# A transformer layer on one core: the first feed-forward input's last column groups in 512-column products, and the ada rows moved away from their end

## The chip, the cores and the metric

The kernel runs on one core of one Trainium2 chip. The core has a matrix engine (TensorE, PE in the profile, with its weight load shown as PEld), a vector engine (VectorE, DVE), a scalar engine (ScalarE, ACT), GpSimd (POOL) and the sync engine SyncE (SP), which here only issues DMAs. Each engine works through its own list of instructions in order and waits on semaphores of the others. The matrix engine writes only to PSUM, which this kernel uses as tiles of 128 x 512 fp32; everything else lies in SBUF.

The metric is the device time in microseconds of one execution. The profile is of one more execution; its times count from the first instruction.

## The reference

One layer, with 256 tokens of width 2048 and a feed-forward width of 5632:

```python
ada = (silu(c) @ w_ada + b_ada)
sh1, sc1, g1, sh2, sc2, g2, sh3, sc3, g3 = split(ada, 9)
h = swiglu(modulate(x, sh1, sc1), ffn1_w_in, ffn1_w_out)
x = layernorm(ALPHA * x + 0.5 * (1 + g1) * h, ln1_g, ln1_b)
h = token_mixer(modulate(x, sh2, sc2), ...)
x = layernorm(ALPHA * x + (1 + g2) * h, ln2_g, ln2_b)
h = swiglu(modulate(x, sh3, sc3), ffn2_w_in, ffn2_w_out)
x = layernorm(ALPHA * x + 0.5 * (1 + g3) * h, ln3_g, ln3_b)

def swiglu(h, w_in, w_out):
    gate, up = split(h @ w_in, 2)
    return (silu(gate) * up) @ w_out
```

Everything is fp32. The change is in the first `swiglu`, in its product with `ffn1_w_in` (2048 x 11264), and in when the pieces of `silu(c) @ w_ada` (2048 x 18432) are worked out.

## The kernel before

**Products in three parts.** Weights and activations are split into a high and a low part (`split`, L154 to L156: a cast on ACT gives the high part, a subtraction on DVE the low one), and a product is high x high + high x low + low x high. In `mm3` (L433) these are three matmuls into one PSUM range. With the weights as the stationary operand and 256 tokens as the moving one, each has 256 columns. In `mm2` (L439) the high weights meet the high and low activations, which lie side by side in one tile, in one matmul of 512 columns; its output fills a whole PSUM tile (high products left, low products right), and a second matmul of 256 columns adds low weights x high activations to the right half. Whoever empties such a tile must add the two halves.

**The first feed-forward's input.** `first_in` works out the first 12 of the 22 pairs of column groups in an order of its own. The other ten, of 256 gate and 256 up columns each, go through `ffn_in` (L458, called at L1075). Loop: group j from 12 to 21; in it gu = 0 (gate columns) and gu = 1 (up columns, called the value group here); `cols_form_a` (L444) then loads two pieces of 1024 x 256 weights (1 MB, `load_w`, one DMA on SP, raw buffer of three), splits each in two halves (six hi and six lo buffers), and issues the products, 8 k x 2 blocks for each piece. `outs[f].shape` decides between `mm2` and `mm3`. Without `values`, as at L1075, gate and up share two PSUM tiles of a group (256 columns each), and after both, silu on ACT (L474) and a multiplication on DVE (L475) empty them. With `values`, as in the second feed-forward (L1710), gate and up each take two whole tiles; a copy on ACT (L464) and an addition on DVE (L465) empty each, then follow silu (L488) for the gate and the multiplication (L485) for the up part. `values` is a pool with the place for the up part (tile u). `mm_tile` hands out five PSUM tiles in turn.

**The first feed-forward's output.** `out_proj` (L494) follows: columns 0 to 1023 in 22 units of two k, then twice 512 columns in 11 units of four k. The first pass needs four PSUM tiles. The last four units are loaded, but their products are held back for the boundary that follows (normalization, modulation, first products of the mixer).

**Ada rows.** `silu(c) @ w_ada` is worked out beside all this by `AdaQueue` (L219): a unit is 1024 columns in 16 rows; a row (`ada_rows`, L186) is a DMA of 128 x 1024 weights (0.5 MB, on SP's queue like the weights, two araw buffers) and one multiply-add on DVE (L170). After the sixteenth row comes a tail of five steps (splits, a sum over partitions on PE, L183, and the placing on DVE, L200 to L204 or L215). The next unit with the usual accumulator cannot begin while such a tail runs. The order is set by hand:

- `pump(n)`, called after a piece of weights, does one step of a tail and issues rows until what is owed is below one; n rows are added to what is owed.
- `half_step`, called by `load_w` between the two halves of a piece, issues half of the last pump's n ahead of time.
- `rest()` sets what is owed, and the rate, to zero.
- `need(n)` forces units until n are done.

The rates are R_F (first input, last quarter, nine pumps), R_IN (ffn_in), R_OUT (out_proj of the first feed-forward) and others (L814). Before the boundary after the first feed-forward `need(6)` (L1093) stands: gate 2 (two units) and shift and scale of the mixer (four). In the last value group the pumps are left out (`last`, L460) and made up for by two pumps behind the loop (L489); the rows of `half_step` still come in between. In the last four units of out_proj there are only steps of tails.

The tile framework orders the instructions of each engine by the program's order and its own estimates; `pinned()` keeps the ada rows behind certain instructions.

Of the kernel before, what the change touches and what calls it, by code (L numbers as in the profile page):

```python
# [9 lines left out]
AF = mybir.ActivationFunctionType  # L10
ALU = mybir.AluOpType
# [4 lines left out]
T = 256  # L16
# [16 lines left out]
def layer_kernel(  # L33
# [8 lines left out]
    V, S, G_, PE, SP = nc.vector, nc.scalar, nc.gpsimd, nc.tensor, nc.sync  # L42
# [23 lines left out]
    def fifth_tile(name):  # L66
        return pm.tile([P, 512], F32, tag="m5", name=name)

    def mm_tile(name, four=False):
        turn[0] = 0 if four else turn[0] % 5 + 1  # L70
        if turn[0] == 5:
            return fifth_tile(name)
        return pm.tile([P, 512], F32, tag="mm", bufs=4, name=name)
# [70 lines left out]
    pin = {}  # L144
# [74 lines left out]
    class AdaQueue:  # L219
# [55 lines left out]
        def pump(self, n):  # L275
            self.owed += n - self.given
            self.rate, self.given = n, 0
            self.end_step()
            self.owed_rows()
# [12 lines left out]
    ada = AdaQueue()  # L292
# [94 lines left out]
    def new_xT(tag):  # L387
        x = xp.tile([P, KD, 2, T], F32R, name=f"x_{tag}")
        return x[:, :, 0], x[:, :, 1], x


    def load_w(src, nk, w, name, by_parts=False, behind=None, into=None):
        raw = wp.tile([P, nk, w], F32, tag="raw", bufs=3, name=f"raw_{name}")
        src = src.rearrange("(k p) n -> p k n", p=P)
        if not by_parts:
            SP.dma_start(raw, src)
        h = nk // 2 if nk * w <= 2048 else nk // 4
        for q in range(nk // h):
            if by_parts:
                SP.dma_start(raw[:, q * h:(q + 1) * h], src[:, q * h:(q + 1) * h])  # L400
            if into:
                hi, los = into[q]
                S.copy(hi, raw[:, q * h:(q + 1) * h, :])
                n = h // len(los)
                for i, lo in enumerate(los):
                    pin["w"] = V.tensor_tensor(out=lo, in0=raw[:, q * h + i * n:q * h + (i + 1) * n, :],
                                               in1=hi[:, i * n:(i + 1) * n, :].bitcast(F32), op=ALU.subtract).ins
                for kk in range(h):
                    yield q * h + kk, hi[:, kk, :], los[kk // n][:, kk % n, :]
                continue  # L410
            if q:
                ada.half_step()
            hi = wp.tile([P, h, w], F32R, tag="hi", bufs=6, name=f"hi_{name}{q}")
            lo = wp.tile([P, h, w], F32R, tag="lo", bufs=6, name=f"lo_{name}{q}")
            with ExitStack() as s:
                if behind:
                    s.enter_context(tc.issue_after(behind))
                pin["w"] = split(raw[:, q * h:(q + 1) * h, :], hi, lo).ins
            for kk in range(h):
                yield q * h + kk, hi[:, kk, :], lo[:, kk, :]  # L420
# [6 lines left out]
    def unwoven(ps):  # L427
        return ps.rearrange("p (n a) -> p a n", a=2)

    def halves(v):  # L430
        return v.rearrange("p (a n) -> p a n", a=2)

    def mm3(o, ah, al, bh, bl, start, stop):  # L433
        bh, bl = woven(bh), woven(bl)
        PE.matmul(o, ah, bh, start=start, stop=False)  # L435
        PE.matmul(o, ah, bl, start=False, stop=False)  # L436
        PE.matmul(o, al, bh, start=False, stop=stop)  # L437

    def mm2(o, ah, al, x, start, stop):  # L439
        PE.matmul(o, ah, x.rearrange("p s (a n) -> p s n a", a=2), start=start, stop=False)  # L440
        PE.matmul(o[:, T:], al, woven(x[:, 0]), start=False, stop=stop)  # L441


    def cols_form_a(src, c0, outs, xT, name, npump, khs=(0, 1)):  # L444
        xhi, xlo, x = xT
        for kh in khs:
            for k8, hi, lo in load_w(src[kh * 1024:(kh + 1) * 1024, c0:c0 + 256], 8, 256, f"{name}_{kh}"):
                k = kh * 8 + k8
                for f in range(2):
                    fs = slice(f * P, (f + 1) * P)  # L450
                    start, stop = k == 8 * khs[0], k == 8 * khs[-1] + 7
                    if outs[f].shape[-1] == 2 * T:
                        mm2(outs[f], hi[:, fs], lo[:, fs], x[:, k], start, stop)
                    else:
                        mm3(outs[f], hi[:, fs], lo[:, fs], xhi[:, k, :], xlo[:, k, :], start, stop)
            npump()

    def ffn_in(w, xT, hT, j0, tag, npump, values=None):  # L458
        def one(j, gu, outs):
            last = gu and j == DFF // 256 - 1  # L460
            cols_form_a(w, gu * DFF + j * 256, outs, xT, f"{tag}i{j}_{gu}", (lambda: None) if last else npump)

        def both(dst, ps):
            S.copy(dst, unwoven(ps[:, :T]))  # L464
            V.tensor_tensor(out=dst, in0=dst, in1=unwoven(ps[:, T:]), op=ALU.add)  # L465

        for j in range(j0, DFF // 256):
            if values is None:
                ps = [mm_tile(f"gu_{tag}{j}_{f}") for f in range(2)]
                for gu in range(2):  # L470
                    one(j, gu, [p[:, gu * T:(gu + 1) * T] for p in ps])
                for f in range(2):
                    h = halves(hT[:, 2 * j + f, :])
                    S.activation(h, unwoven(ps[f][:, :T]), AF.Silu)  # L474
                    pin["h"] = V.tensor_tensor(out=h, in0=h, in1=unwoven(ps[f][:, T:]), op=ALU.mult).ins  # L475
                continue
            for gu in range(2):
                ps = [mm_tile(f"gu_{tag}{j}_{gu}{f}") for f in range(2)]
                one(j, gu, ps)
                for f in range(2):  # L480
                    h = halves(hT[:, 2 * j + f, :])
                    if gu:
                        u = halves(values.tile([P, T], F32, tag="u", bufs=2, name=f"u_{tag}{j}_{f}"))
                        both(u, ps[f])
                        pin["h"] = V.tensor_tensor(out=h, in0=h, in1=u, op=ALU.mult).ins  # L485
                    else:
                        both(h, ps[f])
                        S.activation(h, h, AF.Silu)  # L488
        for _ in range(2):  # L489
            npump()  # L490


# [312 lines left out]
    def entry_of(load, got, u0, u1):  # L805
        for u in range(u0, u1):
            got[u] = []
            for item in load(u):
                got[u].append(item)
                yield  # L810

    R_F, R_IN, R_OUT, R_MX, R_A, R_B = 1.25, 1.2, 1, 1.26, 1, .7  # L814
    NP = 2
    right = dict(side="right")
    def at(rate):
        return lambda: pump(rate)
# [18 lines left out]
    hT = Rows(hp, "hT1")  # L837
# [3 lines left out]
    xT = new_xT("f1")  # L841
    W1 = ffn1_w_in[0]
# [127 lines left out]
    NS = 12  # L970
# [99 lines left out]
    def first_hi_places(tag):  # L1070
        ent["hi0"] = tc.alloc_tile_pool(name=f"hi0{tag}", bufs=1)
        ent["hi"] = [ent["hi0"].tile([P, 2, T], F32R, name=f"hi{tag}_{k}") for k in range(0, 8, 2)]

    first_hi_places("1")
    ffn_in(W1, xT, hT, NS, "f1", at(R_IN))  # L1075
    xp.release()
    need(2)
    W = w_in[0]
# [58 lines left out]
    xT = new_xT("mx")  # L1137
    raws = [mo_raw(u) for u in range(3)]
    mow = {}
    fence, _, xs, ws = boundary(*ent["f"], ent["lgb"], 3, "1", xT, entry_of(mo_load, mow, 3, 6), KD, raws)  # L1140
# [14 lines left out]
    xhi, xlo, _ = xT  # L1155
# [83 lines left out]
    def form_a_four(c0, name, before_last=lambda: None):  # L1239
        ps = [mm_tile(f"pr_{name}{i}", True) for i in range(2)]  # L1240
        for u in range(4):
            if u == 3:
                before_last()
            for k4, hi, lo in load_w(W[u * 512:(u + 1) * 512, c0:c0 + 512], 4, 512, f"{name}{u}",
                                     behind=decays[0]):
                k = 4 * u + k4
                for f in range(4):
                    fs = slice(f * P, (f + 1) * P)
                    mm3(ps[f // 2][:, f % 2 * T:(f % 2 + 1) * T], hi[:, fs], lo[:, fs], xhi[:, k, :], xlo[:, k, :],
                        k + f % 2 == 0, k + f % 2 == KD)  # L1250
            decays[:] = decays[1], None
            step()
        return [ps[f // 2][:, f % 2 * T:(f % 2 + 1) * T] for f in range(4)]
# [279 lines left out]
    for i, c0 in enumerate((C_MQ, C_MK)):  # L1533
        ps = form_a_four(c0, f"m{i}")
# [82 lines left out]
    xT = new_xT("f2")  # L1617
# [13 lines left out]
    hT = Rows(hp, "hT2")  # L1631
# [46 lines left out]
    for us in (0, 1), (2,):  # L1678
        for q in QS:
            last = q == QS[-1]  # L1680
# [28 lines left out]
    vals = tc.alloc_tile_pool(name="vals2", bufs=1)  # L1709
# [45 lines left out]
```

## Time and profile before

| | us |
|---|---|
| median of three runs | 1869.42 |
| lowest and highest of them | 1862.72, 1870.07 |
| profiled execution | 1865.56 |
| its span, first to last instruction | 1863.9 |

The stages by the starts of their products in the trace: first input, first 12 groups, 34.6 to 306.4 us; its last ten groups (`ffn_in`, tiles gu_f, x_f, hi_f1i, lo_f1i) 306.4 to 523.5; the first output (tiles o_f, hi_f1o) 523.5 to 761; the mixer; the second input, of which `ffn_in` with `values` (hi_f2i) 1413.5 to 1624.9; the second output to the end.

How to read the rows: a group or timeline row names engine, line of kernel.py, operation, tiles as out<-in with buffer numbers left out, shape and count; in brackets or behind a bar stand the idle time of the engine just before and what ended it. A timeline row begins with its start and its length in us. A row by tile gives shortest, median and longest duration in ns, then the first and last start. The matmuls overlap, so a matmul's own duration is longer than the step from one to the next; the step is read from starts or from a stage's length.

### The profile page before, as it was taken

The numbers are of one execution on the slowest core, as the hardware profiler recorded it, in microseconds if no ns is written. First come the engines' busy times: TensorE is split into PE (matmuls) and PEld (weight loads), VectorE is DVE, ScalarE is ACT, GpSimd is POOL, SyncE is SP. The second block draws the span as 40 slices with busy tenths as digits, with TensorE's granted clock in tenths as the row PEclk, the third lists the DMA queues.
The fourth block names the chain that finished last, engine by engine and source line by source line (L and its number), as shares of the span: only waits on it lengthen the run. The fifth ranks groups of instructions, "written<-read, shape, count | busy, mean of one in ns | idle before, by whom it ended". The sixth has DMA issues, their size and how long they took to land.

```text
span 1863.9 us, 30963 instructions
## 1 busy us (share of the span) xinstructions
PE 1830.1 (98%) x12521; PEld 1694.2 (91%) x12521; DVE 1455.8 (78%) x1819; ACT 913.5 (49%) x1290; POOL 62.1 (3%) x92
## 2 busy tenths in 40 slices
PE   7999999999999999999999999999999999999997
PEld 5999999999988888689999887999999999988887
DVE  6889989778788787778889878777998776574655
ACT  3554454443454434655566645545454444554441
POOL 1211200000000000000000000000000000000000
PEclk9999999999999999999999999999999999999999
DMA  9989978999897889389978883998878876666663
GB/s 366 383 278 316 319 236 283 321 322 318 285 324 273 311 296 326 129 283 330 313 275 293 324 290 131 343 324 271 293 255 275 273 251 201 198 202 204 204 203 144
DMA packets 263431, 510.82 MB, mean 274 GB/s; under 512 B 10834, under 2 KB 93426, under 8 KB 262264
## 3 DMA queue, kind: packets, MB, share of 16 engines
q1 hardware_dynamic: 255176, 477.90, 74.9%
q0 software_dynamic: 8112, 30.95, 4.8%
q8 instruction: 98, 1.61, 0.4%
q14 instruction: 45, 0.37, 0.1%
HBM read 506.71 MB, written 2.10 MB: 273 GB/s over the span
## 4 chain that ended last, share of the span: by engine, by line
PE 56%; DVE 2%; DMA 1%; issue 1%; ACT 0%; POOL 0%; DVEq 0%; ACTq 0%; POOLq 0%
PE gu_f L440 8%; PE o_f L435 4%; PE o_f L437 4%; PE o_f L436 4%; PE fh L435 4%; PE fh L437 4%; PE fh L436 4%; PE gu_f L441 4%; PE o_mx L435 1%; PE o_mx L436 1%; PE o_mx L437 1%; PE b_mv L435 1%; PE pr_m L435 1%; PE b_mv L436 1%; PE b_mv L437 1%; PE pr_m L437 1%
## 5 line engine op out<-in xcount | busy, mean ns | idle before, releaser
L170 DVE SCALAR_TENSOR_TENSOR acc<-ar,csil,acc 128x1024 f32<-128x1024 f32 (+1 forms) x167 | 211.8, 1269 | 65.7 <-DMA ar<-in_w_ada_dram 65.1
L435 PE MATMUL s<-x_f,hi_s 128*128 128x256 f32 x768 | 211.7, 276 | 1.3 <-DVE hT L1014 1.1
L437 PE MATMUL s<-x_f,lo_s 128*128 128x256 f32 x768 | 211.3, 275 | 0.9 <-DVE lo_s L156 0.7
L436 PE MATMUL s<-x_f,hi_s 128*128 128x256 f32 x768 | 211.4, 275 | 0.0
L440 PE MATMUL gu_f<-x_f,hi_f2i 128*128 128x512 f32 x640 | 209.9, 382 | 0.0
L435 PE MATMUL fh<-x_f,hi_fh 128*128 128x256 f32 x640 | 176.2, 275 | 0.0
L437 PE MATMUL gu_f<-x_f,lo_f1i 128*128 128x256 f32 x640 | 176.0, 275 | 0.0
L437 PE MATMUL fh<-x_f,lo_fh 128*128 128x256 f32 x640 | 176.0, 275 | 0.0
L436 PE MATMUL gu_f<-x_f,hi_f1i 128*128 128x256 f32 x640 | 176.0, 275 | 0.0
L436 PE MATMUL fh<-x_f,hi_fh 128*128 128x256 f32 x640 | 176.0, 275 | 0.0
L435 PE MATMUL gu_f<-x_f,hi_f1i 128*128 128x256 f32 x640 | 176.0, 275 | 0.0
L441 PE MATMUL gu_f<-x_f,lo_f2i 128*128 128x256 f32 x640 | 174.4, 273 | 0.0
L156 DVE TENSOR_TENSOR lo_f2o<-raw_f2o,hi_f2o 128x1024 fp32r<-128x1024 f32 x86 | 105.3, 1225 | 86.7 <-ACT hi_f2o L155 86.6
L155 ACT CAST hi_s<-raw_s 128x1024 fp32r<-128x1024 f32 x96 | 99.5, 1051 | 127.7 <-PE s L436 80.0
L155 ACT CAST hi_f1o<-raw_f1o 128x1024 fp32r<-128x1024 f32 x86 | 89.3, 1048 | 122.0 <-PE o_f L437 73.7
L435 PEld LDWEIGHTS s<-x_f,hi_s 128*128 128x128 f32 x768 | 147.3, 192 | 1.6 <-DVE hT L1014 1.3
L437 PEld LDWEIGHTS s<-x_f,lo_s 128*128 128x128 f32 x768 | 147.4, 192 | 1.2 <-DVE lo_s L156 1.2
L436 PEld LDWEIGHTS s<-x_f,hi_s 128*128 128x128 f32 x768 | 147.4, 192 | 0.4 <-DVE x_f L352 0.4
L155 ACT CAST hi_f2o<-raw_f2o 128x1024 fp32r<-128x1024 f32 x86 | 90.0, 1047 | 115.6 <-PE o_f L437 111.2
L156 DVE TENSOR_TENSOR lo_f2i<-raw_f2i,hi_f2i 128x1024 fp32r<-128x1024 f32 x80 | 97.9, 1224 | 49.2 <-ACT hi_f2i L155 48.6
L440 PEld LDWEIGHTS gu_f<-x_f,hi_f2i 128*128 128x128 f32 x640 | 121.0, 189 | 16.9
L435 PE MATMUL o_f<-hi_f1o,hi 128*128 128x512 f32 x344 | 131.8, 383 | 3.3 <-DVE hT L475 3.3
(444 smaller groups left out, 5254.1 us busy)
## 6 DMA issues: line engine op xcount, KB each, us to landing
ar<-in_w_ada_dram SPq DMA_DIRECT2D x230, 512.0 KB, 5.6
raw_s<-in_ffn_w_in_dram SPq DMA_DIRECT2D x47, 1024.0 KB, 7.4
raw_f1o<-in_ffn_w_out_dram SPq DMA_DIRECT2D x44, 1024.0 KB, 7.3
raw_f2o<-in_ffn_w_out_dram SPq DMA_DIRECT2D x44, 1024.0 KB, 5.2
raw_f1i<-in_ffn_w_in_dram SPq DMA_DIRECT2D x40, 1024.0 KB, 7.7
raw_fh<-in_ffn_w_in_dram SPq DMA_DIRECT2D x40, 1024.0 KB, 6.5
raw_f2i<-in_ffn_w_in_dram SPq DMA_DIRECT2D x40, 1024.0 KB, 5.1
ar<-in_w_ada_dram POOLq DMA_DIRECT2D x45, 512.0 KB, 6.8
```

The costliest lines, as they stand in the source:

```text
L155: S.copy(hi, src)
L156: return V.tensor_tensor(out=lo, in0=src, in1=hi.bitcast(F32), op=ALU.subtract)
L170: V.scalar_tensor_tensor(out=acc, in0=raw, scalar=csil[:, k:k + 1], in1=acc, op0=ALU.mult, op1=ALU.add)
L435: PE.matmul(o, ah, bh, start=start, stop=False)
L436: PE.matmul(o, ah, bl, start=False, stop=False)
L437: PE.matmul(o, al, bh, start=False, stop=stop)
L440: PE.matmul(o, ah, x.rearrange("p s (a n) -> p s n a", a=2), start=start, stop=False)
L441: PE.matmul(o[:, T:], al, woven(x[:, 0]), start=False, stop=stop)
```

## The change

`ffn_in` of the first feed-forward is given a `values` pool, so that its products go through `mm2`; the branch without `values` goes. At the loads of the last value group `ada.rest()` is called there, and the two pumps behind the loop are left out. R_F goes from 1.25 to 1.15 and R_OUT from 1 to 1.06.

```diff
-    def ffn_in(w, xT, hT, j0, tag, npump, values=None):
+    def ffn_in(w, xT, hT, j0, tag, npump, values):
         def one(j, gu, outs):
             last = gu and j == DFF // 256 - 1
+            if last and tag == "f1":
+                ada.rest()
             cols_form_a(w, gu * DFF + j * 256, outs, xT, f"{tag}i{j}_{gu}", (lambda: None) if last else npump)
...
         for j in range(j0, DFF // 256):
-            if values is None:
-                ps = [mm_tile(f"gu_{tag}{j}_{f}") for f in range(2)]
-                for gu in range(2):
-                    one(j, gu, [p[:, gu * T:(gu + 1) * T] for p in ps])
-                for f in range(2):
-                    h = halves(hT[:, 2 * j + f, :])
-                    S.activation(h, unwoven(ps[f][:, :T]), AF.Silu)
-                    pin["h"] = V.tensor_tensor(out=h, in0=h, in1=unwoven(ps[f][:, T:]), op=ALU.mult).ins
-                continue
             for gu in range(2):
                 ps = [mm_tile(f"gu_{tag}{j}_{gu}{f}") for f in range(2)]
                 one(j, gu, ps)
...
-        for _ in range(2):
+        for _ in range(2 * (tag != "f1")):
             npump()
...
-    R_F, R_IN, R_OUT, R_MX, R_A, R_B = 1.25, 1.2, 1, 1.26, 1, .7
+    R_F, R_IN, R_OUT, R_MX, R_A, R_B = 1.15, 1.2, 1.06, 1.26, 1, .7
...
     first_hi_places("1")
-    ffn_in(W1, xT, hT, NS, "f1", at(R_IN))
+    vals = tc.alloc_tile_pool(name="vals1", bufs=1)
+    ffn_in(W1, xT, hT, NS, "f1", at(R_IN), vals)
+    vals.release()
     xp.release()
```

## The prediction

> **What bounds the kernel now.** I read the page first, from its head down to the chain of work that ended last.
>
> ```profile
> span 1863.9 us, 30963 instructions
> PE 1830.1 (98%) x12521; PEld 1694.2 (91%) x12521; DVE 1455.8 (78%) x1819; ACT 913.5 (49%) x1290; POOL 62.1 (3%) x92
> PE 56%; DVE 2%; DMA 1%; issue 1%; ACT 0%; POOL 0%; DVEq 0%; ACTq 0%; POOLq 0%
> ```
>
> TensorE is busy for 1830 of 1864 us and the chain runs through it. So an edit pays only if it shortens TensorE's own stream or one of its few holes. "Busy" does not say at what pace, therefore I put the stage that changes (the last ten column groups of the first input product) beside its twin in the second feed-forward, which already has the form that the change brings. Columns of the stage view: length, then busy time and instructions of PE, weight load, DVE, ACT, POOL, then granted clock, DMA share, GB/s.
>
> ```profile
> 306.40:523.50 217.10, 217.10 (x1934) 216.59 (x1933) 167.33 (x172) 91.31 (x110) 1.08 (x2) 1.00 0.94 309
> 1413.50:1624.90 211.40, 211.40 (x1291) 194.20 (x1289) 144.05 (x168) 103.23 (x144) 0.54 (x1) 1.00 0.72 236
> ```
>
> Both do the same work without a hole in PE: 10 groups x 2 halves x 16 k x 2 blocks = 640 triples of products. The first needs 1920 matmuls of 256 columns (plus 14 others), the second 640 of 512 and 640 of 256 (plus 11). Next the end of each stage, as the same 11.3 us after it, and PE's timeline there.
>
> ```profile
> 523.60:534.90 11.30, 7.97 (x25) 6.20 (x24) 10.73 (x12) 6.10 (x11) 0.00 (x0) 0.70 0.96 354
> 1624.90:1636.20 11.30, 11.30 (x55) 9.90 (x54) 9.40 (x13) 11.30 (x20) 0.00 (x0) 1.00 0.60 197
> ```
>
> ```profile
> 525.29 0.38 PE L437 MATMUL o_f<-hi_f1o,lo 128*128 128x512 f32 x1
> 529.00 0.79 PE L435 MATMUL o_f<-hi_f1o,hi 128*128 128x512 f32 x1 [3.33 <-DVE hT L475]
> 529.59 0.63 PE L436 MATMUL o_f<-lo_f1o,hi 128*128 128x512 f32 x1
> ...
> 534.71 0.45 PE L436 MATMUL o_f<-lo_f1o,hi 128*128 128x512 f32 x1
> 534.99 0.38 PE L437 MATMUL o_f<-hi_f1o,lo 128*128 128x512 f32 x1
> ```
>
> In 11.3 us the first stage's successor starts 25 matmuls, the second's 55. PE stands still for 3.33 us, waiting for DVE's L475, and then runs 14 matmuls (529.00 to 534.71) at half clock, until 534.99. The wait has this cause: the output product takes four PSUM tiles, three are free, and the fourth is the first tile of the last group, which L475 empties. On DVE, L475 stood behind these:
>
> ```profile
> 523.21 1.28 DVE L170 SCALAR_TENSOR_TENSOR acc<-ar,csil,acc 128x1024 f32<-128x1024 f32 x1 [0.59 <-DMA ar<-in_w_ada_dram]
> ...
> 525.06 1.28 DVE L170 SCALAR_TENSOR_TENSOR acc<-ar,csil,acc 128x1024 f32<-128x1024 f32 x1 [0.57 <-DMA ar<-in_w_ada_dram]
> 526.26 2.35 DVE L156 TENSOR_TENSOR lo_f1o<-raw_f1o,hi_f1o 128x1024 fp32r<-128x1024 f32 x2
> 528.53 0.42 DVE L475 TENSOR_TENSOR hT<-hT,gu_f 128x256 f32<-128x256 f32 x1
> ```
>
> Two ada rows that waited for their DMA, and two splits.
>
> **The change, part by part.** (1) *Products.* 640 triples of 256 columns become 640 pairs of 512 and 256; 640 matmuls and weight loads go, the columns streamed stay. From the two stage rows: 217.1 - 211.4 = 5.7 us, 8.9 ns for each triple. The nearest row is the very same form with the same tiles, so I take 5.7; the ends are 0 (PE held by its supply, below) and 5.7. The Trainium skill, "TensorE: Matmul & The Clock Gate", section "Wait — 56ns, not 53.3ns?", speaks against this size: a warm matmul costs its columns at 2.4 GHz plus about 2.5 ns, so 640 fewer would give an estimated 1.6 us; the stage rows do not agree (8.9 ns each), and the sum goes by the rows.
>
> (2) *Empties.* Each of 40 tiles now has a copy on ACT and an addition on DVE; silu (20) and multiplication (20) remain. The second feed-forward shows them:
>
> ```profile
> L464 ACT COPY hT<-gu_f x20: 352/369/375, 1423.8 to 1615.8; 128x256 f32<-128x256 f32 x20
> L465 DVE TENSOR_TENSOR hT<-hT,gu_f x20: 412/417/423, 1424.2 to 1616.8; 128x256 f32<-128x256 f32 x20
> ```
>
> That is 40 x 0.369 = 14.8 us more on ACT (91 + 15 of 211, half idle) and 40 x 0.417 = 16.7 us more on DVE. A tile is wanted again a whole half group (some 10.5 us) after its last product, so PE does not wait for these. Two small tiles come for u; they cost no instruction.
>
> (3) *Ada rows.* Going through the pump's arithmetic (rate per load of 1 MB, half of it between the load's halves, whole rows only, none while an accumulator's tail runs) I count, before and after: 11 and 10 rows ahead of this stage (9 pumps: 11.25 or 10.35), 48 and 45 in it (40 pumps at 1.2 are 48; 38 are 45.6, so 55.95 in all, of which the fraction is dropped), and the remaining 37 and 41 in the output product (room for 40 x 1 or 40 x 1.06); 96, the six units that are due, in both. Each row is a DMA of 0.5 MB on SP's queue and an L170 on DVE:
>
> ```profile
> L170 DVE SCALAR_TENSOR_TENSOR acc<-ar,csil,acc 128x1024 f32<-128x1024 f32 x29 | 37.2, 1283 | 20.5 <-DMA ar<-in_w_ada_dram 20.4
> L155 ACT CAST hi_f1i<-raw_f1i 128x1024 fp32r<-128x1024 f32 x76 | 77.5, 1049 | 105.6 <-DMA raw_f1i<-in_ffn_w_in_dram 85.1 <-PE gu_f L436 10.3 <-PE gu_f L437 4.7
> ```
>
> A row costs 1.28 us on DVE and, at the stage's 309 GB/s for a share of 0.94, 0.52 MB / 329 GB/s = 1.6 us of all DMA engines. In this stage DVE gets 167.3 + 16.7 - 3 x 1.28 = 180 us of work for 211, and DMA the same rate as now (67.1 MB less 1.6, in 5.7 us less: 310 GB/s). The four further rows of the output product (5.1 us of DVE, 6.4 of DMA) lie beside PE work: PE has no hole there at any DVE or DMA load, also where the DMA share is highest.
>
> ```profile
> 540.00:600.00 60.00, 60.00 (x279) 52.48 (x278) 51.93 (x56) 28.28 (x32) 0.00 (x0) 1.00 0.81 279
> 660.00:720.00 60.00, 60.00 (x280) 52.50 (x279) 51.07 (x49) 24.24 (x24) 0.00 (x0) 1.00 0.95 325
> ```
>
> I cost them at nothing; without that cover they are 5 us.
>
> (4) *The boundary.* From the last value group's loads up to the end of the first unit of the output product no row is issued, so none stands before its addition. That addition must come within nine products of PE (nine were done before it stopped). The twin:
>
> ```profile
> 1624.77 0.37 ACT L464 COPY u_f<-gu_f 128x256 f32<-128x256 f32 x1 [1.31 <-PE gu_f L441]
> 1625.18 0.42 DVE L465 TENSOR_TENSOR u_f<-u_f,gu_f 128x256 f32<-128x256 f32 x1 [0.46 <-ACT u_f L464]
> ```
>
> The tile is free at 1625.60; nine products at 0.215 us (60 / 279) after 1624.9 end at 1626.8, 1.2 us later. Behind one cast (1.05) and one split (1.2) it would be 1 us late, a wait of under a third of today's. I take it as gone. What goes: 15 steps from 525.29 to 534.99 take 9.7 us and should take 15 x 0.215 = 3.2; 6.5 us.
>
> (5) *Supply of the split weights in the faster stage.* Today PE never waits here, but its margin is small.
>
> ```profile
> L435 PE MATMUL gu_f<-x_f,hi_f1i x640: 270/275/275, 306.4 to 523.2; 128*128 128x256 f32 x160
> L156 DVE TENSOR_TENSOR lo_f1i<-raw_f1i,hi_f1i x80: 1216/1221/1229, 301.5 to 513.0; 128x1024 fp32r<-128x1024 f32 x80
> 436.29 1.22 DVE L156 TENSOR_TENSOR lo_f1i<-raw_f1i,hi_f1i 128x1024 fp32r<-128x1024 f32 x1
> ```
>
> There are 80 half loads of 24 matmuls, 2.71 us each. The first is split at 302.7, 3.7 us ahead of its use; the one split at 437.5 is the fiftieth, used at about 306.4 + 49 x 2.71 = 439.2: 1.7 us ahead; the last at 514.2, used at 520.5: 6 us ahead. By the fiftieth, PE will be 49 x 0.07 = 3.4 us earlier; one row fewer ahead of the stage gives 1.3 to 1.6 back; two additions may stand before a split (0.8). 1.7 - 3.4 + 1.5 - 0.8 = -1.0: a wait of 1 us. Ends: 0 (DVE's 50 us of idle time takes all), and 13 (none of it: rival C). I take 1.0.
>
> **Sum:** -5.7 - 6.5 + 1.0 = -11.2 us. The profiled execution took 1865.6 (1.7 more than its span); that gives 1854.4. The three other runs lie at 1862.7, 1869.4 and 1870.1, their median 3.9 above the profiled one. I go from 1867.5, half way: 1856 us, 0.6% faster. About 0.5%, 9.3 us, is what a measurement of this kernel can tell from no change.
>
> **Rivals.** *A, the stage stays at 217 us:* its supply, not PE, sets the pace. For it: DMA share 0.94, and casts that wait 85 us for DMA. Against: 0.95 with PE full at 660 to 720 us. Then only the boundary pays: -6.5, 1861.0. Chance 0.15, with a matmul count that hardly matters. (By the Trainium skill's 2.5 ns of part 1 the estimate would be 1859.4 without a wait.) *B, the boundary keeps its wait:* the addition, now behind a copy on ACT, comes late behind other work. Against: the twin, though with fewer rows about. -5.7 + 1.0: 1862.8. Chance 0.10. *C, slower:* DVE becomes the bound of the stage. ACT and DVE work in order, and each addition waits for a copy that can stand behind a cast that waits for DMA; today's case of it:
>
> ```profile
> 314.11 1.05 ACT L155 CAST hi_f1i<-raw_f1i 128x1024 fp32r<-128x1024 f32 x1 [3.65 <-DMA raw_f1i<-in_ffn_w_in_dram]
> ...
> 315.48 0.45 DVE L1014 TENSOR_TENSOR hT<-s,gate 128x256 f32<-128x256 f32 x1 [2.38 <-ACT s L1013]
> ```
>
> If DVE's idle 49.8 us stay, the stage takes 180 + 50 = 230: +13 - 6.5; and if the 13 us fall into four waits of 3.3, each followed by the half clock seen at 529 (3.2 us): +19 in all, 1887. It is slower than before from a stage of 223.6 us on, by 0.5% from 233. Without loss of clock it is +6.5, 1874. Chance 0.07. (The Trainium skill, "TensorE: Matmul & The Clock Gate", section "Why this matters for your kernels", puts the loss of clock at gaps of over some 3 us; the 3.33 us at 525 agree, and no row here shows what shorter ones inside a product stream do.) *D, the six units end late:* row 96 now comes in the last columns' sixth unit and the five steps of its tail end with the eleventh, the last; DVE's cover there is
>
> ```profile
> 745.42 0.17 DVE L204 TENSOR_TENSOR scsh<-scsh,bcol 128x8 f32<-128x8 f32 x1
> 751.32 0.70 DVE L553 TENSOR_TENSOR o_f<-o_f,gate 128x512 f32<-128x512 f32 x1 [5.72 <-PE o_f L437]
> ```
>
> 5.7 us. Two units later (2 x 24 products, 10.3 us) in the order is 4.6 past it at worst: -6.6, 1860.9. Chance 0.04.
>
> **Range and chances.** Forecast 0.64 (1856). From the lowest run less a full 12.2 (no wait in the stage): 1850; from the highest less B's least gain, 5.7: 1864. Outside are C and the tails. Faster by over 0.5%: 0.58 (a tenth of the forecast's cases fall short of 9.3); slower: 0.05 (most of C); the rest 0.37.
>
> **What would show it.** Right: the stage at 211 to 213 us with some 1290 PE instructions, PE's waits there under 2 us; no wait before the first o_f and clock 1.00 after it; DVE near 180 us in the stage; PE full from there to 740. Wrong: gu_f matmuls waiting for lo_f1i (C, A), a wait of o_f for L465 (B), or PE waiting for a bc or DVE ending L204 after the first held products (D).

## The result, and the profile after

The changed kernel is slower: 1876.67 us, the median of 15 runs (1871.17 to 1882.34), against 1864.73 us for the kernel before (15 runs, 1859.97 to 1874.99). The ratio is 1.0059, with a 95% interval of 1.0045 to 1.0073. The profiled execution grew by 11.1 us, from a span of 1863.9 to one of 1875.0, so the two traces can be set side by side.

The head of the page after, with busy time and instructions of each engine, and the shares of the chain that ended last:

```profile
span 1875.0 us, 29749 instructions
PE 1828.4 (98%) x11881; PEld 1673.8 (89%) x11881; DVE 1471.0 (78%) x1859; ACT 924.3 (49%) x1330; POOL 62.6 (3%) x92
PE 55%; DVE 2%; DMA 1%; issue 1%; ACT 1%; POOL 0%; DVEq 0%; ACTq 0%; POOLq 0%; SPq 0%
```

The 640 matmuls are gone (12521 to 11881) and PE is busy 1.7 us less, yet the span is longer. So what was lost is time in which PE stands still. The windows of after show where; the columns are as in the prediction (length, then busy time of PE, weight load, DVE, ACT and POOL, clock, DMA share, GB/s).

```profile
305.70:523.50 217.80, 214.19 (x1295) 195.18 (x1293) 180.53 (x209) 100.81 (x148) 1.36 (x2) 1.00 0.94 308
523.50:534.80 11.30, 10.35 (x49) 8.76 (x48) 10.95 (x14) 11.02 (x19) 0.00 (x0) 1.00 0.97 345
640.00:735.00 95.00, 92.88 (x430) 80.96 (x430) 75.87 (x81) 38.73 (x39) 1.06 (x2) 1.00 0.86 293
735.00:745.00 10.00, 3.09 (x15) 2.33 (x13) 2.43 (x3) 1.54 (x2) 0.00 (x0) 0.80 1.02 392
745.00:755.00 10.00, 6.26 (x15) 5.04 (x16) 7.66 (x10) 2.96 (x4) 0.00 (x0) 0.51 0.77 259
```

The first row is the changed stage: 217.8 us, where 217.1 stood before, although its products are now the shorter form. The second row is the boundary behind it: 49 matmuls start where 25 did. The third has a hole of 2.1 us. In the last two, some 30 matmuls run in 20 us. The waits of PE name the holes (engine, line and tile, what was waited for; us in total, times, longest):

```profile
PE bc L183 <- ACT ahi L155: 10.6, 1, 10.6
...
PE gu_f L440 <- DVE hT L467: 3.5, 3, 1.2
...
PE o_f L435 <- DVE res L548: 2.1, 1, 2.1
...
PE o_f L435 <- DVE u_f L467: 1.0, 1, 1.0
```

**The large hole.** PE's timeline of after, and behind it ACT's; the second number is the duration, and in brackets stand the idle time before and what ended it:

```profile
736.16 0.40 PE L183 MATMUL bc<-ahi,trir 128*128 128x512 f32 x1
...
737.71 0.38 PE L437 MATMUL o_f<-dhi,lo 128*128 128x512 f32 x1
748.74 0.79 PE L183 MATMUL bc<-ahi,trir 128*128 128x512 f32 x1 [10.65 <-ACT ahi L155]
749.33 0.63 PE L435 MATMUL o_f<-dhi,hi 128*128 128x512 f32 x1
...
754.45 0.52 PE L437 MATMUL o_f<-hi_f1o,lo 128*128 128x512 f32 x1
754.81 0.38 PE L435 MATMUL o_f<-hi_f1o,hi 128*128 128x512 f32 x1
```

```profile
726.53 0.62 ACT L155 CAST ahi<-acc 128x512 fp32r<-128x512 f32 x1
...
743.46 1.99 ACT L155 CAST hi_f1o<-raw_f1o 128x1024 fp32r<-128x1024 f32 x2 [9.24 <-DMA raw_f1o<-in_ffn_w_out_dram]
746.18 1.99 ACT L155 CAST hi_f1o<-raw_f1o 128x1024 fp32r<-128x1024 f32 x2 [0.73 <-DMA raw_f1o<-in_ffn_w_out_dram]
748.07 0.61 ACT L155 CAST ahi<-acc 128x512 fp32r<-128x512 f32 x1
```

The sum over partitions of the sixth unit's second half (bc) is a small matmul. It waits for a cast (ahi) whose data had been there since the first half was cast at 726.5, and whose one buffer came free when PE read the first half, at 736.16. But ACT works in its order, and in that order the cast stands behind the casts of the last two loads of weights. These landed late, so the cast came late, and behind bc stand PE's held products. Of the four held units the first two had their operands; those of the last two came with the late loads themselves (their splits end on DVE between 746.9 and 750.2). So without bc in between PE would have stood for a shorter time, but not for none: an estimate from these rows puts the add-up of the last columns (DVE's first step that empties their PSUM tile) at 752 to 753 us (the last split, and the six products behind it, some of them at half clock). It came at 761.5, and at the pace of before it would have come at 748.4. The order was the same before, on PE and on ACT; only the loads came sooner. The same casts in ACT's timeline of before:

```profile
735.25 1.99 ACT L155 CAST hi_f1o<-raw_f1o 128x1024 fp32r<-128x1024 f32 x2 [3.48 <-DMA raw_f1o<-in_ffn_w_out_dram]
...
740.26 0.61 ACT L155 CAST ahi<-acc 128x512 fp32r<-128x512 f32 x1
```

Why the loads came late is on the queues. SP's timeline of after and then of before (an x2 or x4 groups several issues; the second number runs from the first to the last of them):

```profile
725.17 1.78 SPq L189 DMA_DIRECT2D ar<-in_w_ada_dram  x2
732.92 2.21 SPq L396 DMA_DIRECT2D raw_f1o<-in_ffn_w_out_dram  x2
```

```profile
714.79 0.37 SPq L189 DMA_DIRECT2D ar<-in_w_ada_dram  x1
717.72 13.81 SPq L396 DMA_DIRECT2D raw_f1o<-in_ffn_w_out_dram  x4
```

Before, the last row was issued at 714.8 and the last weights by 731.5. After, the last two rows are issued from 725.2 on, and the last weights from 732.9 to 735.1, because SP had to wait 5.9 us for the split (L156) that frees a raw buffer. (In both kernels these rows belong to the seventh unit and are fetched ahead.) The first of these weights ended ACT's wait at 743.46, 10.5 us after its issue, while the DMA engines were at a share of 1.02 (row 735 to 745 above). Before, the same load was issued at 730.1 and ended ACT's wait at 735.25, 5.2 us later. The gain and bias of the normalization, 1 MB each, now also go ahead of the last weights: in POOL's timeline the first is issued at 731.48, and at 734.42 before, behind them.

**The small holes in the stage.** DVE's timeline of after at the first of the three waits for L467:

```profile
382.02 1.28 DVE L170 SCALAR_TENSOR_TENSOR gate<-ar,csil,gate 128x1024 f32<-128x1024 f32 x1
383.21 1.22 DVE L156 TENSOR_TENSOR lo_f1i<-raw_f1i,hi_f1i 128x1024 fp32r<-128x1024 f32 x1
388.70 1.28 DVE L170 SCALAR_TENSOR_TENSOR gate<-ar,csil,gate 128x1024 f32<-128x1024 f32 x1 [4.27 <-DMA ar<-in_w_ada_dram]
389.90 1.22 DVE L156 TENSOR_TENSOR lo_f1i<-raw_f1i,hi_f1i 128x1024 fp32r<-128x1024 f32 x1
391.04 1.28 DVE L170 SCALAR_TENSOR_TENSOR gate<-ar,csil,gate 128x1024 f32<-128x1024 f32 x1
392.23 0.74 DVE L467 TENSOR_TENSOR hT<-hT,gu_f 128x256 f32<-128x256 f32 x2
```

The copies of the two tiles had been made on ACT at 385.4 and 386.6. The additions that empty them ran at 392.2: ahead of them on DVE stood a row that waited 4.27 us for its DMA, with a split and a further row behind it. PE wanted the tile at 391.55 and got it at 392.70.

**The account**, from the starts of the same products in both traces: the stage begins 0.7 us earlier and takes 0.6 longer; the boundary gives 5.2 (24 more matmuls at 0.216 us in the same 11.3 us); the hole at 642.5 takes 2.1 and a little more; from the 951st product of the output (ten before the first held one) to the add-up of the last columns it is 27.5 us for 14.4, or +13.1; the rest of the kernel adds 0.9. Together +11.

### The profile page after: what moved, and what is told of

It reads as the page before. It is cut to its first block, busy times and chain, and to the rows that moved or that the text cites. A ratio compares the mean times of both kernels' runs of the same rounds, so it can differ in the third digit from the quotient of the medians.

```text
span 1875.0 us, 29749 instructions
## 1 busy us (share of the span) xinstructions
PE 1828.4 (98%) x11881; PEld 1673.8 (89%) x11881; DVE 1471.0 (78%) x1859; ACT 924.3 (49%) x1330; POOL 62.6 (3%) x92
## 4 chain that ended last, share of the span: by engine, by line
PE 55%; DVE 2%; DMA 1%; issue 1%; ACT 1%; POOL 0%; DVEq 0%; ACTq 0%; POOLq 0%; SPq 0%
PE gu_f L440 7%; PE o_f L436 4%; PE o_f L435 4%; PE o_f L437 4%; PE fh L435 4%; PE fh L437 4%; PE fh L436 4%; PE gu_f L441 4%; PE o_mx L437 1%; PE o_mx L436 1%; PE o_mx L435 1%; PE b_mv L435 1%; PE b_mv L436 1%; PE pr_m L435 1%; PE b_mv L437 1%; PE pr_m L436 1%
## 5 line engine op out<-in xcount | busy, mean ns | idle before, releaser
L440 PE MATMUL gu_f<-x_f,hi_f1i 128*128 128x512 f32 x640 | 210.6, 383 | 3.6 <-DVE hT L467 3.5
L437 PE MATMUL s<-x_f,lo_s 128*128 128x256 f32 x768 | 211.4, 276 | 0.9 <-DVE lo_s L156 0.7
L436 PE MATMUL s<-x_f,hi_s 128*128 128x256 f32 x768 | 211.4, 275 | 0.0
L440 PE MATMUL gu_f<-x_f,hi_f2i 128*128 128x512 f32 x640 | 209.9, 382 | 0.0
L156 DVE TENSOR_TENSOR lo_f2o<-raw_f2o,hi_f2o 128x1024 fp32r<-128x1024 f32 x86 | 105.2, 1225 | 86.8 <-ACT hi_f2o L155 86.6
L440 PEld LDWEIGHTS gu_f<-x_f,hi_f1i 128*128 128x128 f32 x640 | 120.9, 189 | 21.3 <-DVE hT L467 4.4
L156 DVE TENSOR_TENSOR lo_f2i<-raw_f2i,hi_f2i 128x1024 fp32r<-128x1024 f32 x80 | 97.8, 1223 | 49.9 <-ACT hi_f2i L155 49.1
```

The lines of the kernel that those rows point to most:

```text
L156: return V.tensor_tensor(out=lo, in0=src, in1=hi.bitcast(F32), op=ALU.subtract)
```

## The experiments

The theory after this reading: the rows that were moved into the output product make the tail of the sixth unit late, and the new products are innocent. The rivals: the new form itself costs the time (its empties on ACT and DVE), or the last loads are late for another reason (the normalization's gain and bias ahead of them). The table has every kernel that ran. Ratios are to the kernel before in runs on the same chip; the last four columns are of the one profiled execution, in us: its time, the stage (first product of the ten groups to first product of the output), the output up to its 951st product, and from there to the add-up. Executions of one kernel lie up to 17 us apart, so a time is judged by median and interval, and a trace tells what waited.

| kernel | median | ratio [95%] | profiled | stage | to 951st | to add-up |
|---|---|---|---|---|---|---|
| before | 1864.73 | 1 | 1865.56 | 217.2 | 213.4 | 14.4 |
| after | 1876.67 | 1.0059 [1.0045, 1.0073] | 1876.67 | 217.8 | 210.5 | 27.5 |
| e1 products only | 1864.86 | 1.0000 [0.9983, 1.0016] | 1864.48 | 213.7 | 215.0 | 14.0 |
| e2 rows only | 1872.39 | 1.0043 [1.0025, 1.0061] | 1871.33 | 217.8 | 209.5 | 25.2 |
| e3 R_OUT 1.15 | 1871.55 | 1.0036 [1.0015, 1.0056] | 1864.64 | 218.3 | 210.2 | 17.9 |
| e4 gain, bias behind | 1870.38 | 1.0030 [1.0006, 1.0053] | 1877.87 | 218.1 | 215.5 | 21.2 |
| e5 rows early | 1864.71 | 1.0009 [0.9996, 1.0023] | 1866.93 | 216.4 | 216.6 | 12.7 |
| e6 = e5 and e4 | 1864.53 | 1.0000 [0.9986, 1.0015] | 1859.85 | 216.6 | 211.0 | 12.7 |
| e7 = e5, old products | 1864.23 | 1.0007 [0.9992, 1.0022] | 1865.37 | 217.2 | 216.3 | 12.7 |
| e8 no gain, bias | 1871.71 | 1.0048 [1.0029, 1.0067] | 1873.05 | 218.5 | 210.5 | 22.2 |
| e9 after, half rows | 1855.46 | 0.9945 [0.9928, 0.9963] | 1858.94 | 216.2 | 206.9 | 14.0 |
| e10 before, half rows | 1858.66 | 0.9971 [0.9956, 0.9986] | 1863.61 | 218.2 | 206.9 | 14.0 |
| e11 rows early, less so | 1860.28 | 0.9971 [0.9951, 0.9991] | 1856.06 | 215.4 | 209.9 | 12.7 |
| e12 half rows multiplied | 1860.33 | 0.9981 [0.9964, 0.9998] | 1864.04 | 219.7 | 206.9 | 15.8 |

### One half of the change at a time

e1 keeps the new products and undoes all that concerns rows. From the changed kernel:

```diff
-            if last and tag == "f1":
-                ada.rest()
...
-        for _ in range(2 * (tag != "f1")):
+        for _ in range(2):
...
-    R_F, R_IN, R_OUT, R_MX, R_A, R_B = 1.15, 1.2, 1.06, 1.26, 1, .7
+    R_F, R_IN, R_OUT, R_MX, R_A, R_B = 1.25, 1.2, 1, 1.26, 1, .7
```

> The products of the change alone; rates, make-up pumps and rows of before. Theory T (the loss sits at the end of the output product: the last rows and their tail come later, the last weights land late and PE's sum of the tail waits 10.6 us for them): the tail ends two units earlier again, no wait of PE over 1 us there; the stage of ten groups takes 217 to 220 us (4.8 us less of matmuls, 5 to 8 of waits), the wait at the start of the output product is back; in all within 0.3% of before. Theory M (the copies and additions of the 512-column form slow the whole run): slower than before by 8 us or more, as with the change.

Its windows of the stage and of the boundary, then the wait of PE at the boundary:

```profile
307.20:520.90 213.70, 212.59 (x1294) 195.00 (x1293) 178.21 (x208) 99.15 (x145) 1.07 (x2) 1.00 0.95 310
520.90:532.20 11.30, 5.30 (x19) 4.08 (x18) 10.60 (x13) 7.32 (x12) 0.00 (x0) 0.72 0.94 321
```

```profile
PE o_f L435 <- DVE u_f L465: 6.0, 1, 6.0
```

With the old rows the stage takes 213.7 us, 3.4 less than before: here the products pay, in this execution (I had expected 217 to 220). The boundary takes some of it back. PE comes earlier to an addition that still stands behind rows, and waits 6.0 us for it instead of 3.3. There is no wait for bc, and the last stretch is as before. The median is that of before.

e2 is the other half, the old products with the new rows (`rest`, no make-up pumps, the new rates). From the changed kernel, beside putting the branch without `values` back:

```diff
-    def ffn_in(w, xT, hT, j0, tag, npump, values):
+    def ffn_in(w, xT, hT, j0, tag, npump, values=None):
...
-    ffn_in(W1, xT, hT, NS, "f1", at(R_IN), vals)
+    ffn_in(W1, xT, hT, NS, "f1", at(R_IN))
```

> The rows of the change alone (rest, no make-up pumps, 1.15 and 1.06); products in three matmuls of 256 columns as before. T: the ten groups at 217 us without waits, no wait at the start of the output product (-6.5), but PE's bc waits 8 to 11 us at its end, followed by half clock (+11 to +13): slower than before by 4 to 7 us. M: faster than before by about 6 us, no such wait.

```profile
PE bc L183 <- ACT ahi L155: 8.6, 1, 8.6
```

That wait, from PE's waits of e2, a last stretch of 25.2 us and a time 8 us above before show it: the rows alone make the tail late, without any of the new products. The boundary is mended in e2 as in after (a wait of 1.0). So the two halves are not independent gains. Rows spare the boundary and lose the tail; products gain in the stage only as long as rows and weights come in time.

### What makes the tail late

e3 makes the rows of the output denser; e4 issues gain and bias on SP behind the last weights; e8 leaves them out:

```diff
-    R_F, R_IN, R_OUT, R_MX, R_A, R_B = 1.15, 1.2, 1.06, 1.26, 1, .7
+    R_F, R_IN, R_OUT, R_MX, R_A, R_B = 1.15, 1.2, 1.15, 1.26, 1, .7
```

> The change with R_OUT 1.15 for 1.06: row 96 then comes in the third unit of the last columns instead of the sixth, the tail ends in the eighth instead of the eleventh. T: no wait of bc over 2 us, 10 to 13 us less than the change, 0 to 3 us less than before. M: within 3 us of the change, 8 us or more above before.

```diff
-            SP.dma_start(raw, src)
+            last_load[0] = SP.dma_start(raw, src).ins
...
+                if tag == "f1":
+                    with tc.issue_after(last_load[0]):
+                        ent["lgb"] = ln_params(ln1_g, ln1_b, "1", SP)
...
-        ent["lgb"] = ln_params(g, b, tag, G_)
+        if tag != "1":
+            ent["lgb"] = ln_params(g, b, tag, G_)
```

> The change, with the two 1 MB loads of the norm's gain and bias (lg, lb) issued on SP behind the last weights of the output product instead of on POOL's queue ahead of them. If these two loads are what delays the last weights (in the change they are issued at 731.5 and 732.0, the weights at 732.9 and land 10.5 us later): the weights land within 6 us, the wait of bc falls from 10.6 to under 5 us, 5 to 10 us less than the change. If the lateness of rows alone does it: the wait stays within 2 us of 10.6.

```diff
-        ent["lgb"] = ln_params(g, b, tag, G_)
+        if tag == "1":
+            ent["lgb"] = [lnp.tile([P, D], F32, tag=t, name=f"{t}_{tag}") for t in ("lg", "lb")]
+            G_.memset(ent["lgb"][0], 1.0)
+            G_.memset(ent["lgb"][1], 0.0)
+        else:
+            ent["lgb"] = ln_params(g, b, tag, G_)
```

> The change, without the loads of the first norm's gain and bias (2 MB): lg is set to one and lb to zero, so the gain and bias of that norm are left out. If lg and lb delay the last weights: these land within 6 us, the wait of bc falls from 10.6 to under 3 us, 8 to 12 us less than the change. If they only happen to lie there: the wait stays at 8 us or more.

The waits of PE for the tail, in e3, e4 and e8:

```profile
PE bc L183 <- DVE alo L156: 2.4, 1, 2.4
```

```profile
PE bc L183 <- ACT ahi L155: 4.7, 1, 4.7
```

```profile
PE bc L183 <- ACT ahi L155: 6.1, 1, 6.1
```

Each takes a part of the 10.65 us, and none all of it. e3 met neither expectation: the wait is 2.4 us, and the median fell by 5 us, not by 10. In its trace ACT's order has the second ahi ahead of the last pair of casts, at 735.6. e4 came out as I had said for gain and bias as the cause: a wait under 5 us, and a median 6.3 us below the change. e8 came out between its two cases: 6.1 us of wait stay, where I had looked for less than 3 or for 8 and more. The issue of the load in e8, and the cast that it lets go:

```profile
735.79 2.21 SPq L396 DMA_DIRECT2D raw_f1o<-in_ffn_w_out_dram  x2
```

```profile
741.42 1.99 ACT L155 CAST hi_f1o<-raw_f1o 128x1024 fp32r<-128x1024 f32 x2 [4.32 <-DMA raw_f1o<-in_ffn_w_out_dram]
```

From issue to cast it takes 5.6 us here, 5.4 in e4 and 5.2 before, against 10.5 in after. So the 5 us that this load took longer are those of gain and bias; the two rows fetched ahead lie in front of the weights in all of these runs. What is left of the wait has another reason: the load is issued late for PE, 1.7 us (e8) and 2.5 us (e4) before the 951st product, where it was 6.9 us before. Gain and bias are thus not the whole cause, but some 4.5 to 6 us of the wait. The medians of all three lie between before and after, but the runs of e3 spread over 1864.6 to 1875.0 and those of e4 over 1862.3 to 1878.7, so the share of each is rough.

### The rows brought forward

e5 has the old R_F, many more rows in the output, and puts the seventh unit behind the boundary after the feed-forward in the program's order (`stage=1`). The trace shows that two of its rows are fetched ahead all the same, at 702.8 and 705.2, but now over 20 us before the last weights (726.4 and 728.6):

```diff
-    R_F, R_IN, R_OUT, R_MX, R_A, R_B = 1.15, 1.2, 1.06, 1.26, 1, .7
+    R_F, R_IN, R_OUT, R_MX, R_A, R_B = 1.25, 1.2, 1.3, 1.26, 1, .7
...
-    ada.pair(6, 0)
+    ada.pair(6, 0, stage=1)
```

> The change with R_F 1.25, R_OUT 1.3 and the seventh unit (pair 6, 0) held until after the boundary: the 96 rows end some eight units of the output product earlier, and its last thirteen units are loaded without rows beside them. Theory S (the end of the output product is bound by its last loads, which share DMA with rows, with the rows fetched ahead and with lg and lb; whatever PE gains before it turns into waiting there): waits of PE from 720 us to the first add-up under 2 us, the add-up at 743 to 746 us, 5 to 8 us less than before. Theory D (DMA is the bound of the whole first feed-forward, and rows put earlier only move the waits): PE waits in the middle of the output product instead, total within 3 us of before.

e6 adds the edit of e4, and e7 has these rows with the old products.

> The kernel above, with lg and lb issued on SP behind the last weights. S: as above, and up to 3 us less, since the last weights land in 5 to 6 us; D: no difference.

> The rows as in the first kernel of these four, the products in three matmuls of 256 columns as before. It tells what the 512-column form is worth where the end does not bind. S: 3 to 6 us less than before (the wait at the start of the output product gone), and 1 to 4 us more than with the 512-column form. If the copies and additions cost as much as the matmuls save: equal to it.

In all three the wait for bc is gone and the last stretch falls to 12.7 us, 15 less than in after. In e5 the last of the 96 rows is multiplied at 694.8 instead of 724.6, both sums of the tail stand ahead of the held products (the last at 720.3), and the load of above is issued 12.7 us before the 951st product. So the late end comes of the rows. But theory S fails all the same: none of the three is faster than before, which is what D had said. The new products do not show in the times either: e7 with the old ones is at 1864.23, e5 and e6 at 1864.71 and 1864.53. And in e5 the hole has moved. PE's timeline of e5 at the change from the first output columns to the next:

```profile
643.99 0.77 PE L435 MATMUL o_f<-hi_f1o,hi 128*128 128x512 f32 x1 [4.83 <-DVE res L548]
644.55 0.63 PE L436 MATMUL o_f<-lo_f1o,hi 128*128 128x512 f32 x1
...
648.39 0.57 PE L436 MATMUL o_f<-lo_f1o,hi 128*128 128x512 f32 x1
648.80 0.38 PE L437 MATMUL o_f<-hi_f1o,lo 128*128 128x512 f32 x1
```

The add-up of the first columns, which empties their PSUM tiles, now stands on DVE behind rows, and PE waits 4.83 us and then runs 11 matmuls slowly. In e7 it waits 3.2 there with the old products. So R_OUT has a price on either side: too few rows make the end late, too many hold up the change of columns.

### How much is the supply

e9 leaves out half of the rows of the units 3_0 to 3_3 (32 of the 96) in the changed kernel, e10 in the kernel before; e12 loads them and leaves out only their multiply-adds:

```diff
         for k in range(KD):
+            if k % 2 and tag[:2] == "3_":
+                yield
+                continue
```

> The change, with every second ada row of the mixer's four shift-and-scale units left out (32 rows: their DMA and their multiply-add; the columns' sums are incomplete). Theory D (from 306 to 740 us the supply by DMA and DVE, rows included, is nearly the bound, so that PE's gains are given back as waits wherever the supply falls behind): PE waits from 306 to 760 us fall from 19 us to under 4, the first add-up at 740 to 744 us, 14 to 20 us less than the change, 5 to 9 us less than before. Theory S (only the order at the very end matters): the waits inside the ten groups (3 to 5 us) stay.

> The kernel before, with the same 32 rows left out. D: PE was full here but for the wait at the start of the output product, so at most that goes (0 to 6 us less than before); the difference from the kernel above is what the change is worth with supply to spare: 4.8 us of matmuls and up to 6.5 of that wait.

```diff
-            ada_acc(acc, raw, k)
+            if not (k % 2 and tag[:2] == "3_"):
+                ada_acc(acc, raw, k)
```

> The change, with the same 32 rows loaded but not multiplied (the sums are incomplete): DMA as in the change, 41 us less on DVE. If DMA is the supply's bound: waits of PE and time within 3 us of the change. If DVE's queue is: as with the rows left out altogether, 14 us or more less than the change.

Windows of e9 and of e12 in the output:

```profile
525.00:640.00 115.00, 115.00 (x534) 100.65 (x533) 85.53 (x90) 56.05 (x65) 0.00 (x0) 1.00 0.76 255
```

```profile
525.00:640.00 115.00, 115.00 (x538) 100.73 (x538) 82.43 (x85) 56.75 (x67) 0.00 (x0) 1.00 0.88 301
```

With 32 rows fewer, after drops from 1.0059 to 0.9945, some 21 us, and before only from 1 to 0.9971, 5.4 us. So with supply to spare the change does gain: 1855.46 against 1858.66, 3.2 us (of the 96 pairs of a run of e9 and a run of e10, e9 is faster in 87). With the DMAs kept at a share of 0.88 instead of 0.76 and only DVE relieved (e12), 0.9981 is reached, 14.5 of the 21 us. The multiply-adds are thus the larger part of the trouble and the traffic the smaller one; the result lies between my two cases (3 us or less, and as much as in e9). It is not shown that this is DVE's queue alone: a row that nothing multiplies does not hold its araw buffer until DVE comes to it, and the load of above is issued 6.9 us before the 951st product in e12, against 1.1 in after. e12 also starts the tail one row sooner, since its last row is among those left out; how much of the 14.5 these two are was not tried. PE's waits for bc are not all gone in e12: 1.6 us at the end, and 2.5 us at 435 within the stage.

### A version that gains

e11 is e6 with R_OUT at 1.2 in place of 1.3: the new products, `rest()` at the boundary, the old R_F, the seventh unit behind the boundary in the program's order (two of its rows are fetched at 701.2 and 706.7), gain and bias behind the last weights.

```diff
-    R_F, R_IN, R_OUT, R_MX, R_A, R_B = 1.15, 1.2, 1.06, 1.26, 1, .7
+    R_F, R_IN, R_OUT, R_MX, R_A, R_B = 1.25, 1.2, 1.2, 1.26, 1, .7
```

> The change with R_F 1.25, R_OUT 1.2, the seventh unit held until after the boundary, and lg and lb behind the last weights: between the two rates tried. D: no wait over 3 us at either end of the output product in most runs, 0 to 4 us less than before; no version with all rows gains the full 11 us.

PE's waits of e11 between 300 and 750 us that reach 1 us, and its window of the boundary:

```profile
PE o_f L437 <- DVE res L550: 1.3, 1, 1.3
PE gu_f L442 <- DVE hT L469: 1.1, 1, 1.1
```

```profile
520.00:531.30 11.30, 11.02 (x52) 9.34 (x51) 10.66 (x13) 9.86 (x17) 0.00 (x0) 1.00 0.94 350
```

1860.28 us, 0.9971 [0.9951, 0.9991]: faster than before by about 5 us by the ratio (3.5 between the medians on this chip), and than after by 16. In its trace no wait of more than 1.3 us is left in these stages, the stage is at 215.4, the boundary starts 52 matmuls where 25 stood, and the last stretch takes 12.7. The old products with these rows were not run, so it is not shown that the new ones have a part in this gain; e7 beside e5 and e6 shows none.

## Why the prediction was wrong

I forecast 1856 us with a range to 1864. The time was 1876.67, and the kernel got slower. The starting point of 1867.5 was close to the later median of 1864.73; the error is in the sum, -11.2 against +11.1 in the profiled executions, 22.3 us. By the prediction's steps:

- **(1) Products, -5.7: right in kind, too large by a sixth.** The starts of the 640 triples and pairs step by 0.3350 and 0.3275 us on average, 4.8 us in all. Most of the other 0.9 was not the form: beside its products the twin has 11 matmuls, this stage 14. The prediction's estimate from the Trainium skill, "TensorE: Matmul & The Clock Gate", section "Wait — 56ns, not 53.3ns?", was 1.6 us; it is further off than the twin. In the time of the whole kernel the gain does not show (e1, e7) unless rows are left out (e9 against e10).
- **(2) Empties, "PE does not wait for these": failed.** The half group of some 10.5 us was right as cover: the tile of the first hole had its last product at 379.9 and was wanted at 391.55. But the copy on ACT came 5 us after that product and the addition on DVE nearly 7 us after the copy, behind a row that waited for its DMA. I counted the busy time that the additions bring, and not what stands ahead of them. That is rival C's mechanism at the size of 3.5 us in three waits.
- **(3) Ada rows: the count was nearly right, the price was the main failure.** DVE multiplies 10, 47 and 39 rows ahead of the stage, in it and in the output before, and 9, 46 and 41 after. "I cost them at nothing", because PE had no hole at any load of DVE or DMA. The rows that I read this from end at 720 us; they show PE's own work in the middle of the output, where nothing depends on the ada rows. At the end something does. The last row is multiplied at 724.6 instead of 713.5, rows are still issued at 726.5 instead of 714.8, the last weights come late behind them, and the tail must pass through ACT behind these weights. In place of nothing, the end costs 13.1 us. e2 (25.2 us in the last stretch with the rows alone) and e5 to e7 (12.7) show it.
- **(4) The boundary, -6.5: right.** The windows give 5.2; a wait of 0.95 us is left, and the clock holds. e1 shows what stands there if the rows stay: 6.0.
- **(5) Supply of the split weights, +1.0: failed in size and in place.** Four matmuls more than the twin at 0.22 us put an undisturbed stage at 211.4 + 0.9 = 212.3; it took 217.8, so 5.5 are lost. The larger part is the three waits for tiles of (2), not those for splits. Where the rows fall in the groups may matter: with R_F at 1.25 the stage has one such wait (e1, e6, e11) or two (e5), with 1.15 two (e4) or three (after, e3, e8). The margins were read a little small, too: in the trace the fiftieth half load is used at 439.8 and the last at 521.1, not at 439.2 and 520.5.
- **The rivals.** D had the right place, the end of the six units, and the sign that I named for it, PE waiting for a bc. Its mechanism was not what came: it moved the tail two units back in the order, but on PE and ACT the tail stands among the held products and behind the last casts as it did before. What moved is the loads ahead of it. So its price was wrong as well: 4.6 us worked out on DVE's cover before the add-up, where it cost 13.1. DVE's idle time before the add-up was in fact still there afterwards (6.46 us). What waited was PE, on an ACT cast with its data ready and its place in the order behind a late DMA. 10.65 us of waiting and some 12 matmuls at half clock (12 x 0.21 = 2.5) make the 13.1. At that price D is on the side of slower, with more than the 0.04 that I gave it.

What stays open: why the last weights are issued so late. In SP's trace they wait for splits that free a raw buffer, and these splits wait for earlier loads, which share the DMA engines with the rows; how much of this are the rows of the sixth unit and how much the two fetched ahead was not separated, since no run is without the latter.

## What to carry to other kernels

When background work is moved to a later place, price its last item and not its average: follow the chain from its last load through every engine's order to the instruction that the bound engine will meet, and see what stands ahead of it in each queue. A small matmul in PE's order whose operand passes through a busy queue is a gate for all products behind it. An added instruction that empties a buffer costs what is queued ahead of it, not its 0.4 us, so where such an instruction must come in time, no work that waits for DMA may be put in front of it.

## What the runs showed of the hardware

PE's clock did not follow the length of a stop alone. Stops of 1.09 us (before, at 301.27), 2.12 (after, 642.55), 2.23 (e8, 531.27) and 3.03 (e1, 302.04) kept it. Stops of 2.19 us (e4, 531.23) and of 3.33, 4.83, 6.00 and 10.65 us were followed at once by 7 to 14 matmuls at half rate (durations of 0.63 us in the timelines mark half rate, 0.38 full rate). In e3 a stop of 2.4 us was followed by four matmuls at full rate and only then by eight at half. In after three stops of 1.15 us kept the clock; in e4 one, close behind a stop of 0.60 us, lost it, and again only after six matmuls:

```profile
396.78 0.48 PE L442 MATMUL gu_f<-x_f,hi_f1i 128*128 128x512 f32 x1 [1.15 <-DVE hT L469]
...
398.35 0.63 PE L442 MATMUL gu_f<-x_f,hi_f1i 128*128 128x512 f32 x1
```

The granted clock tells more. In the body of the kernel each spell at half clock lasts 3.41 us or two, three or four times that. The five of e4 begin at 234.17, 398.01, 531.13, 650.59 and 749.58 us, which are 48, 39, 35 and 29 steps of 3.41 us apart. So in these traces the clock changes on a fixed grid. Two windows of e4 along its grid, around the stops above, and two of e1, around its stop of 3.03 us (its grid is that of its spell at 525.87):

```profile
394.60:398.01 3.41, 1.66 (x9) 1.34 (x9) 3.41 (x5) 1.25 (x3) 0.00 (x0) 1.00 0.87 220
398.01:401.42 3.41, 3.41 (x13) 2.87 (x12) 3.12 (x4) 3.41 (x5) 0.00 (x0) 0.50 0.70 228
```

```profile
297.20:300.61 3.41, 1.81 (x17) 1.62 (x15) 1.06 (x4) 2.19 (x4) 0.00 (x0) 1.00 0.74 265
300.61:304.02 3.41, 1.98 (x17) 1.98 (x18) 3.41 (x6) 0.54 (x1) 0.00 (x0) 1.00 0.93 294
```

In e4 PE was busy for 0.49 of a step, and the next step ran at half clock. In e1 the longer stop fell on two steps, busy for 0.53 and 0.58, and the clock stayed. From 240 to 760 us each of the 14 losses in these runs followed a step in which PE was busy for at most 0.49 of it, and no step above a half was followed by one; one step at 0.47 kept the clock as well (e6, at 297.4). Earlier in the kernel losses followed busier steps (0.59 in e4, at 230.8), which this does not explain.

The Trainium skill, "TensorE: Matmul & The Clock Gate", section "What's actually happening", says that activity is judged in windows of about 3.4 us that run freely. The spells of 3.41 us and their grid agree with that. For an estimate this means that a stop of 1 to 3 us may cost its length, or its length and some 1.7 us more for each step at half clock.
